# The second mixer of a two-layer trunk: gate products on quarters of the array, ScalarE in the order of issue, and two channel tiles of the output projection tile by tile

## The chip, the cores and the metric

The kernel runs on one core of one Trainium2 chip, in one launch. The metric is the device time in microseconds (us). The kernel before took 1646.99 us (median of three runs, 1646.67 to 1647.06). Its profile comes from one more execution, which took 1642.21 us and whose recorded span is 1640.4 us, with a mean granted TensorE clock of 0.997.

The engines have short names in the profile: PE is TensorE (PEld its weight load), DVE is VectorE, ACT is ScalarE, POOL is GpSimd, and SP is SyncE, which here only issues DMAs.

## The reference

The model has two layers on 256 context tokens and 256 latent tokens with 1024 channels. A layer is a half-step SwiGLU feed-forward block, a mixer, and a second feed-forward block, each between two norms. The change concerns the mixer of the second layer, which gives out latent tokens only. Of its heads it needs three groups, cut here to their core:

```python
# recurrent heads: 512 channels; r, i, a, bx for two directions d, then a linear scan each way
r  = sigmoid(einsum('blhi,hij->blhj', xh, w_r[d]) + b_r[d])     # heads of 64 channels: 64 x 64 blocks
i  = sigmoid(einsum('blhi,hij->blhj', xh, w_i[d]) + b_i[d])
log_a = -8.0 * r * softplus(-lam[d]);  a = exp(log_a)
bx = sqrt(-expm1(2.0 * log_a)) * (i * xf)
h[t] = a[t] * h[t-1] + bx[t]            # context first, then latent; d == 1 runs backward
o_lru = gelu(lru_gate) * (h_forward + h_backward)
# short convolution: 256 channels                # chunk mixing: 256 channels, chunks of 128 tokens
o_sc = sc_bg * conv3(sc_cg * sc_x)
o_cm = gelu(cm_u) * (einsum('hpq,bnqhd->bnphd', ws, gelu(cm_v)) + bs)
out  = concatenate([o_lru, o_sc, o_cm]) @ w_mix_out
```

## The kernel before, in words

Channels lie on the 128 partitions and tokens along the free axis, so 1024 channels are eight channel tiles. A product of the input projection is taken as three: each fp32 weight tile and each activation tile is split into a rounded part `hi` (a cast on ScalarE, line 173) and a rest `lo` (a subtraction on VectorE, line 174), and hi·hi, hi·lo and lo·hi are added. The 2304 projected columns come as 16 units of 128 columns and, for the value half of the chunk mixing, two units that hold half of the contraction each for 256 columns. A unit of 128 is loaded by one DMA, cast by two instructions, subtracted by two, and then takes 24 TensorE instructions.

The middle of the second mixer is a list of parts in ORDER[1], each a letter and a number. `mixer` calls them in that order:

- `c`, `x`, `b`: the three products of a short convolution half, with its work on VectorE (lines 759 to 787).
- `C`: the four-tap convolution of a recurrent channel tile over all 512 tokens (lines 701 and 703).
- `G`: the gates of that tile. Its weights `wbd` are block-diagonal 128 x 128 fp32 matrices of two 64-channel heads; four products of 512 columns each (two directions, r and i), a sigmoid each on ScalarE (lines 719 and 723), and a multiplication on VectorE (724).
- `D`: the decay, exp and tanh on ScalarE (730, 731) and three VectorE instructions per direction (732, 734, 735).
- `S`: root (ScalarE, 741), root times input (742), scans (744, 747, 748), sum and gate (750, 751) on VectorE. The result is one of the inputs `oh[0]` to `oh[3]` of the output projection.
- `v`, `u`, `m`: the chunk mixing. `v` is the value product with two gelus (798), `u` a unit with a gelu (805), `m` a product with `wcm`, an addition and a multiplication on VectorE (816, 818). Its results are `oh[6]` and `oh[7]`; those of the short convolution are `oh[4]` and `oh[5]`.
- `w` loads the output weights of one of eight output tiles; `p` issues the four products of one output tile with `oh[4]` to `oh[7]`.

Behind the list come the products of LATE[0] with that channel tile for all eight output tiles (`out_part`). Then, output tile by output tile, follow the products of LATE[1] and, for each tile, three ScalarE passes over its result (899 to 901), a VectorE product `c` (903), sums, and products with `ones` into `st`, from which the norm is made. After these comes the next feed-forward block.

Two things set the order of the instructions on an engine. For the engines in MANUAL (before: TensorE alone) the instructions stand in the order in which the code issues them. For the other engines a scheduler picks the order when the program is built, and it is then fixed: each engine works through its own list, and an instruction at the head that waits holds all behind it. Each ScalarE function that is in another table than the one loaded costs an ACT_TABLE_LOAD: sigmoid, exp with tanh, gelu and root each bring one when they follow another.

Weights are loaded by SP; `raw` tiles have four buffers (NRAW), split tiles six (NSPL).

Of the kernel before, what the change touches and what calls it, by code (L numbers as in the profile page):

```python
# [34 lines left out]
PARK = {2: 2, 3: 3, 6: 0, 7: 1}  # L35
NTMP = 3
NSQ = 3
JACC = 'gvg'
FIRST = 2

# [3 lines left out]

OUT_AT = ((0, 0), (0, 1), (1, 0), (1, 1), (2, 0), (3, 0), (4, 0), (5, 0))

LATE = ((0,), (1, 2, 3))
MANUAL = {mybir.EngineType.PE}

ORDER = ("c1 C0 g3 G0 C1 C2 C3 D0 c0 x1 G1 G3 D3 x0 S0 D1 v0 S3 G2 b0 g2 D2 u0 m0 S1 b1 u1 m1 S2",  # L50
         "c0 x0 C1 C0 C3 C2 g3 g2 G1 G0 D1 D0 c1 b0 u0 v0 S1 w0 G3 u1 x1 b1 m1 w1 S0 m0 G2 w2 p1 w3 w4 w5 p2 p5 w6 D2 S2 w7 p0 "
         "D3 S3 p7 p4 p3 p6")

TAIL = 4

# [26 lines left out]
def backbone(ctx: ExitStack, tc: tile.TileContext, xT, vecs, crow, w_mod, w_in, w_out, w_mi, w_mo, w_lru, w_cm, b_cm, lam, w_last, out):  # L82
    nc = tc.nc
# [12 lines left out]
    def nm(s):  # L96
        cnt[0] += 1
        return f"{s}_{cnt[0]}"
# [4 lines left out]
    def pbank():  # L103
        return ps.tile([P, 512], F32, tag="mm", name=nm("mm"))
# [525 lines left out]
    def mixer(l, segs, nxt, plan, skew_out, order_of, next_unit=None):  # L630
# [77 lines left out]

        def lru_conv(c):
            xcs[c] = conv(c)  # L710

        def lru_gates(c):
            wbd = tp.tile([P, 4, P], F32, tag="wbd", name=nm("wbd"))
            nc.sync.dma_start(wbd, w_lru[l, c])
            for c, d, b in heads[2 * c:2 * c + 2]:
                pr = pbank()
                pe.matmul(pr, lhsT=wbd[:, 2 * d, :], rhs=xcs[c], start=True, stop=True)
                r = rs[c, d] = tt_()
                sc.activation(r, pr, AF.Sigmoid, bias=V("b_r", b))
                pi = pbank()  # L720
                pe.matmul(pi, lhsT=wbd[:, 2 * d + 1, :], rhs=xcs[c], start=True, stop=True)
                i = ix[c, d] = tt_()
                sc.activation(i, pi, AF.Sigmoid, bias=V("b_i", b))
                ve.tensor_tensor(i, i, xcs[c], op=OP.mult)

        def lru_decay(c):
            for c, d, b in heads[2 * c:2 * c + 2]:
# [7 lines left out]
                ve.tensor_scalar(e, e, -1.0, 1.0, op0=OP.mult, op1=OP.add)  # L735
                es[c, d] = e

        def lru_scan(c):
            for c, d, _ in heads[2 * c:2 * c + 2]:
                e, h, b = es[c, d], rs[c, d], ix[c, d]  # L740
                sc.activation(h, h, AF.Sqrt, scale=-1.0)
                ve.tensor_tensor(b, b, h, op=OP.mult)
                if d == 0:
                    ve.tensor_tensor_scan(h, e, b, 0.0, op0=OP.mult, op1=OP.add)
                else:
                    r1, r2 = slice(SEQ - 1, None, -1), slice(T - 1, SEQ - 1, -1)
                    ve.tensor_tensor_scan(h[:, r1], e[:, r1], b[:, r1], 0.0, op0=OP.mult, op1=OP.add)
                    ve.tensor_tensor_scan(h[:, r2], e[:, r2], b[:, r2], h[:, 0:1], op0=OP.mult, op1=OP.add)
            h = rs[c, 1]
            ve.tensor_tensor(h[:, a0:b0], h[:, a0:b0], rs[c, 0][:, a0:b0], op=OP.add)  # L750
            ve.tensor_tensor(h[:, a0:b0], h[:, a0:b0], gates[c][:, a0:b0], op=OP.mult)
            put(c, h)

        sc_o, sc_p = {}, {}

# [86 lines left out]
        def out_part(k):  # L842
            for m in range(KT):
                out_mm(m, (k,))

        parts = dict(w=out_load, p=lambda m: out_mm(m, (4, 5, 6, 7)), g=gate, c=short_c, x=short_x, b=short_b, v=lambda _: chunk_v(), u=chunk_u, m=chunk_mix,
                     C=lru_conv, G=lru_gates, D=lru_decay, S=lru_scan)
        def issue():
            for part in order_of.split():
                parts[part[0]](int(part[1]))  # L850

        if len(segs) == 2:
            with tc.manual_schedule(engines=MANUAL):
                issue()
            norms = Norms(segs, None, l, 1, nxt)
            order = [4, 5, 6, 7, 0, 1, 2, 3]
            y = norms.y = [tt_() for _ in range(KT)]

            def load(m):
# [11 lines left out]
        need(l, 8)  # L871
        need(nxt[0], 3 * nxt[1])
        need(nxt[0], 3 * nxt[1] + 1)
        with tc.manual_schedule(engines=MANUAL):
# [376 lines left out]
```

## Time and profile before

| | |
|---|---|
| median of three runs | 1646.99 us |
| the profiled execution | 1642.21 us, its span 1640.4 us |
| PE busy | 1612.5 us, 98% of the span |
| DVE, ACT, POOL busy | 1164.3, 736.7, 120.3 us |
| the chain that ended last | PE 89%, DVE 6%, ACT 3% of the span |
| HBM traffic | 247.39 MB read, 151 GB/s over the span |

The stretch that the change touches is the second mixer's middle, about 1350 to 1447 us of the span. In these 97 us PE was busy for 92.57, ACT for 80.60 and DVE for 78.28 us, POOL for 6.43.

How to read it: a row of the timeline gives the start in us, the duration in us, engine, line, operation, out<-in by the program's names with buffer numbers left out, shapes, and xN where N instructions of one kind stand in a row and are shown as one; the duration is then that of all N. What stands in brackets is the idle time before and what ended it. On PE an fp32 product of weight and data shows as two instructions. Consecutive instructions of an engine overlap a little, so what one adds to a row of work is the distance between starts.

### The profile page before, as it was taken

What the parts mean: (1) busy time and instruction counts of PE and PEld (TensorE: products, weight loads), DVE (VectorE), ACT (ScalarE), POOL (GpSimd) and SP (SyncE); (2) the same over time, 40 slices, a digit from 0 to 9 for tenths busy, and PEclk for the clock granted to TensorE, in tenths of its full rate; (3) what the DMA queues carried; (4) which work ended last, traced back from release to release, by engine and by line L of the source; (5) the groups of instructions that cost most, each with busy time, mean ns of one, the idle gap of its engine ahead of it and who ended that gap; (6) DMA issues with size and microseconds to landing.
All of it is one profiled execution on the core that took longest, in us unless ns stands there. A gap on an engine that the chain in (4) does not pass through costs nothing.

```text
span 1640.4 us, 23432 instructions
## 1 busy us (share of the span) xinstructions
PE 1612.5 (98%) x8846; PEld 1371.6 (84%) x8846; DVE 1164.3 (71%) x2183; ACT 736.7 (45%) x1378; POOL 120.3 (7%) x166
## 2 busy tenths in 40 slices
PE   6999999999999999999999999999999999999998
PEld 3788888889977998888888998888888998789997
DVE  4899898548788787867763887767432788785554
ACT  5523322244697662332233462332232479864543
POOL 0000000005000500000000410000000410100000
PEclk9999999999999999999999999999999999999999
DMA  9577677431323225655552215655422316155552
GB/s 370 189 218 261 205 229 223 144 121 44 103 72 120 77 97 187 221 162 174 179 164 80 100 61 194 222 166 167 141 90 90 103 54 210 47 167 194 180 191 78
DMA packets 73906, 249.97 MB, mean 152 GB/s; under 512 B 8384, under 2 KB 10048, under 8 KB 73792
## 3 DMA queue, kind: packets, MB, share of 16 engines
q1 hardware_dynamic: 73216, 247.94, 45.9%
q8 instruction: 69, 1.13, 0.3%
q10 hardware_dynamic: 576, 0.52, 0.1%
q14 instruction: 45, 0.37, 0.1%
HBM read 247.39 MB, written 1.05 MB: 151 GB/s over the span
## 4 chain that ended last, share of the span: by engine, by line
PE 89%; DVE 6%; ACT 3%; DMA 1%; issue 1%; POOL 0%; SPq 0%; POOLq 0%; DVEq 0%; ACTq 0%
PE mm L113 87%; PE st L113 1%; DVE x L271 1%; DVE sq L394 1%; DVE t L703 0%; PE mod L113 0%; DVE z L270 0%; DVE tmp L262 0%; DMA x<-in_xT 0%; ACT hi L173 0%; DVE t L397 0%; POOL rs L241 0%; DVE t L332 0%; DMA raw<-in_w_mi 0%; ACT t L730 0%
## 5 line engine op out<-in xcount | busy, mean ns | idle before, releaser
L173 ACT CAST hi<-raw 128x512 fp32r<-128x512 f32 (+1 forms) x596 | 343.6, 610 | 672.7 <-PE mm L113 475.8
L113 PE MATMUL mm<-hh,hi 128*128 128x512 f32 (+1 forms) x1840 | 625.6, 348 | 0.5 <-ACT hh L1095 0.2
L113 PE MATMUL mm<-hl,hi 128*128 128x512 f32 (+1 forms) x1840 | 622.5, 346 | 1.8 <-DVE hl L256 1.0
L174 DVE TENSOR_TENSOR lo<-raw,hi 128x512 fp32r<-128x512 f32 (+1 forms) x596 | 387.5, 680 | 157.3 <-ACT hi L173 154.5
L113 PE MATMUL mm<-hh,lo 128*128 128x512 f32 (+1 forms) x1840 | 466.6, 346 | 0.0
L113 PEld LDWEIGHTS mm<-hh,hi 128*128 128x128 f32 x1840 | 345.5, 188 | 52.1 <-ACT hh L1095 2.8
L113 PEld LDWEIGHTS mm<-hl,hi 128*128 128x128 f32 x1840 | 345.9, 188 | 51.2 <-DVE hl L1101 1.6
L113 PEld LDWEIGHTS mm<-hh,lo 128*128 128x128 f32 x1840 | 325.1, 188 | 47.2
L196 DVE SCALAR_TENSOR_TENSOR junk<-raw,cb 128x1024 bf16<-128x1024 f32 x256 | 312.9, 1222 | 70.8 <-DMA raw<-in_w_mod 67.1
L113 PE MATMUL mm<-t,hi 128*128 128x512 f32 (+1 forms) x1056 | 240.6, 367 | 0.0
L113 PEld LDWEIGHTS mm<-t,hi 128*128 128x128 f32 x1056 | 182.8, 188 | 35.7 <-issue 0.2
L397 POOL TENSOR_TENSOR t<-t,sq 128x256 f32<-128x256 f32 x112 | 94.2, 856 | 712.2 <-ACT sq L391 702.3
L113 PE MATMUL mm<-t,lo 128*128 128x512 f32 (+1 forms) x528 | 131.5, 367 | 0.0
L113 PEld LDWEIGHTS mm<-t,lo 128*128 128x128 f32 x528 | 92.6, 188 | 17.7
L480 DVE TENSOR_TENSOR sg<-sg,mm 128x512 f32<-128x512 f32 (+1 forms) x72 | 45.9, 640 | 78.3 <-PE mm L113 78.3
L113 PE MATMUL mm<-t,hh 128*128 128x256 f32 x512 | 71.2, 281 | 0.0
L113 PEld LDWEIGHTS mm<-t,hh 128*128 128x128 f32 x512 | 65.7, 188 | 0.5
L173 ACT CAST t<-sg 128x512 fp32r<-128x512 f32 (+1 forms) x94 | 50.6, 541 | 32.0 <-DVE sg L480 29.0
L332 DVE TENSOR_TENSOR t<-t,mm 128x256 f32<-128x256 f32 (+1 forms) x66 | 35.4, 536 | 29.3 <-PE mm L113 29.1
L174 DVE TENSOR_TENSOR t<-sg,t 128x512 fp32r<-128x512 f32 (+1 forms) x94 | 55.3, 589 | 0.9 <-ACT t L173 0.9
L113 PE MATMUL mm<-hi,t 128*128 128x512 f32 x176 | 55.1, 394 | 0.0
L263 ACT ACTIVATE hh<-tmp,modv 128x256 fp32r<-128x256 f32 x72 | 42.4, 596 | 22.1 <-DVE tmp L262 21.9
(179 smaller groups left out, 1212.4 us busy)
## 6 DMA issues: line engine op xcount, KB each, us to landing
raw<-in_w_in SPq DMA_DIRECT2D x176, 512.0 KB, 3.6
raw<-in_w_mod SPq DMA_DIRECT2D x128, 512.0 KB, 4.3
raw<-in_w_out SPq DMA_DIRECT2D x48, 512.0 KB, 3.3
raw<-in_w_mi SPq DMA_DIRECT2D x36, 512.0 KB, 4.1
raw<-in_w_last SPq DMA_DIRECT2D x22, 512.0 KB, 3.3
raw<-in_w_out SPq DMA_DIRECT2D x24, 384.0 KB, 3.7
t<-in_w_mod SPq DMA_DIRECT2D x32, 256.0 KB, 5.8
raw<-in_w_mo SPq DMA_DIRECT2D x8, 512.0 KB, 3.7
```

The lines of the kernel that those rows point to most:

```text
L113: te.matmul(dst, lhsT=lhsT, rhs=rhs, start=start, stop=stop)
L173: sc.copy(hi, src)
L174: ve.tensor_tensor(lo, src, hi.bitcast(F32), op=OP.subtract)
L196: ve.scalar_tensor_tensor(junk, raw.rearrange("p k c -> p (k c)"), 1.0, cb[:, s], op0=OP.mult, op1=OP.mult, accum_out=modv[l][:, v, m, s:s ...
L263: sc.activation(hh[:, m, a:b], tmp, AF.Identity, scale=A, bias=B)
L271: ve.scalar_tensor_tensor(x[:, m, a:b], z, mcol(l, 3 * i + 2, m, s), x[:, m, a:b], op0=OP.mult, op1=OP.add)
L332: ve.tensor_tensor(y[m][:, a:b], y[m][:, a:b], p[:, :b - a], op=OP.add)
L394: ve.scalar_tensor_tensor(q[2], y, G, x[:, m, a:b], op0=OP.mult, op1=OP.mult)
L397: (gp if JACC[c] == "g" else ve).tensor_tensor(acc[c], acc[c], q[c], op=OP.add)
L480: ve.tensor_tensor(sg[:, :b - a], sg[:, :b - a], pu[:, :b - a], op=OP.mult)
```

## The change

Three edits, all for the second layer's mixer; the first layer's instructions keep their order on each engine.

1. Gates on quarters. Instead of a block-diagonal 128 x 128 matrix, `gate_products` keeps only the 64 x 64 blocks and issues two products of 64 rows by 64 columns where there was one. Rows of the array are given by g (0 for r, 1 for i), columns by the head h. For two of the four quarters the head's 64 channels lie on the other half of the partitions, so `lru_swap` makes a copy of the channel tile with its halves exchanged, by two DMAs from GpSimd per channel tile. The weights come in by four DMAs per channel tile, where there was one.
2. ScalarE in the order of issue. IN_ORDER adds ScalarE to TensorE for the second layer; VectorE stays with the scheduler. The roots become a part of their own, `R`, and the hand-over to the output projection another, `H`. ORDER[1] is written anew, so that gates, decays, roots and scans of two channel tiles come together; `l4` fills the queue of units to four.
3. LATE: the products with channel tiles 1 and 0 come ahead for all output tiles, those with 3 and 2 tile by tile (before: 0 ahead, and 1, 2, 3 tile by tile).

```diff
-LATE = ((0,), (1, 2, 3))
+LATE = ((1, 0), (3, 2))
 MANUAL = {mybir.EngineType.PE}
+IN_ORDER = {mybir.EngineType.PE, mybir.EngineType.Activation}
...
-         "c0 x0 C1 C0 C3 C2 g3 g2 G1 G0 D1 D0 c1 b0 u0 v0 S1 w0 G3 u1 x1 b1 m1 w1 S0 m0 G2 w2 p1 w3 w4 w5 p2 p5 w6 D2 S2 w7 p0 "
-         "D3 S3 p7 p4 p3 p6")
+         "c0 x0 C1 C0 C3 C2 g3 g2 G1 G0 c1 l4 D1 D0 b0 R1 R0 S1 S0 H1 H0 u0 u1 v0 G3 G2 D3 D2 w0 x1 b1 R3 R2 S3 S2 H3 H2 "
+         "m1 w1 m0 w2 p1 w3 w4 w5 p2 p5 w6 w7 p0 p7 p4 p3 p6")
...
         def lru_conv(c):
             xcs[c] = conv(c)
+            if l in QUARTERS:
+                lru_swap(c)
...
+        def lru_swap(c):
+            t = turned_xc[c] = tp.tile([P, T], F32, tag="swap", name=nm("swap"), bufs=2)
+            for a, b in ((0, P // 2), (P // 2, 0)):
+                gp.dma_start(t[a:a + P // 2], xcs[c][b:b + P // 2])
...
+            if l in QUARTERS:
+                wbd = tp.tile([P, 2, 2, P // 2], F32, tag="wbd", name=nm("wbd"))
+                for g in range(2):
+                    for h in range(2):
+                        a = 64 * h
+                        src = w_lru[l, c].rearrange("p (d g) o -> p d g o", g=2)
+                        nc.sync.dma_start(wbd[64 * g:64 * g + 64, :, h], src[a:a + 64, :, g, a:a + 64])
+            else:
+                wbd = tp.tile([P, 4, P], F32, tag="swap", name=nm("wbd"))
...
+                    for h in range(2):
+                        src = (xcs if g == h else turned_xc)[c]
+                        rows, cols = slice(64 * g, 64 * g + 64), slice(64 * h, 64 * h + 64)
+                        pe.matmul(p[cols], lhsT=wbd[rows, d, h], rhs=src[rows], start=True, stop=True)
...
+        def lru_root(c):
+            for d in range(2):
+                sc.activation(rs[c, d], rs[c, d], AF.Sqrt, scale=-1.0)
+
         def lru_scan(c):
-            for c, d, _ in heads[2 * c:2 * c + 2]:
+            for d in range(2):
                 e, h, b = es[c, d], rs[c, d], ix[c, d]
-                sc.activation(h, h, AF.Sqrt, scale=-1.0)
...
-            put(c, h)
+
+        def lru_put(c):
+            put(c, rs[c, 1])
...
-        with tc.manual_schedule(engines=MANUAL):
+        with tc.manual_schedule(engines=IN_ORDER if l in QUARTERS else MANUAL):
             issue()
             for k in LATE[0]:
                 out_part(k)
-        with tc.manual_schedule(engines=MANUAL2):
+        with tc.manual_schedule(engines=MANUAL2 | IN_ORDER if l in QUARTERS else MANUAL2):
```

In the order rows below, line numbers of the changed kernel are some 3 higher at its top and 36 to 42 higher in the mixer (741 becomes 777, 744 becomes 784, 747 and 748 become 787 and 788, 750 and 751 become 790 and 791, 816 and 818 become 858 and 860, 174 becomes 177); numbers behind a name tell tiles of one name apart.

First place: VectorE from the end of the scans of channel tile 0 on, in the kernel before. `t_12484` and `t_12503` are the two chunk mixes, `oh[7]` and `oh[6]`; 742 is root times input, 783 belongs to a short convolution.

```order
L742 TENSOR_TENSOR t_12149<-t_12149,t_12145 128x512
L783 TENSOR_TENSOR t_12218<-t_12218,mm_12453 128x256
L816 TENSOR_TENSOR t_12484<-mm_12479,bcm 128x256
L744 SCALAR_TENSOR_TENSOR t_12145<-t_12173,t_12149 128x512
L818 TENSOR_TENSOR t_12484<-t_12484,t_12422 128x256
L742 TENSOR_TENSOR t_12158<-t_12158,t_12154 128x512
L816 TENSOR_TENSOR t_12503<-mm_12498,bcm 128x256
L747 SCALAR_TENSOR_TENSOR t_12154<-t_12179,t_12158 128x256
L818 TENSOR_TENSOR t_12503<-t_12503,t_12287 128x256
L748 SCALAR_TENSOR_TENSOR t_12154<-t_12179,t_12154,t_12158 128x256
L750 TENSOR_TENSOR t_12154<-t_12154,t_12145 128x256
```

The same place in the changed kernel, which is the end of the scans of channel tiles 3 and 2. Its chunk mixes are `t_12595` (`oh[7]`) and `t_12605` (`oh[6]`).

```order
L790 TENSOR_TENSOR t_12459<-t_12459,t_12448 128x256
L782 TENSOR_TENSOR t_12488<-t_12488,t_12486 128x512
L791 TENSOR_TENSOR t_12459<-t_12459,t_12096 128x256
L787 SCALAR_TENSOR_TENSOR t_12486<-t_12509,t_12488 128x256
L858 TENSOR_TENSOR t_12595<-mm_12590,bcm 128x256
L788 SCALAR_TENSOR_TENSOR t_12486<-t_12509,t_12486,t_12488 128x256
L860 TENSOR_TENSOR t_12595<-t_12595,t_12366 128x256
L790 TENSOR_TENSOR t_12486<-t_12486,t_12475 128x256
L858 TENSOR_TENSOR t_12605<-mm_12600,bcm 128x256
L791 TENSOR_TENSOR t_12486<-t_12486,t_12131 128x256
L860 TENSOR_TENSOR t_12605<-t_12605,t_12331 128x256
```

Before, the chunk mixes stood between the scans of channel tile 0, ahead of all work of the decays of tiles 2 and 3; now they stand between the last scans of all, and the second one's multiplication is the last row of them.

Second place: VectorE around the rests of the second unit of `v`, in the kernel before. They are the rows of `lo_12257`; the first unit's are those of `lo_12223`, and line 732 begins the first decay.

```order
L174 TENSOR_TENSOR lo_12223<-raw_12220,hi_12222 128x512
L724 TENSOR_TENSOR t_12149<-t_12149,t_12036 128x512
L174 TENSOR_TENSOR lo_12223<-raw_12220,hi_12222 128x512
L174 TENSOR_TENSOR lo_12257<-raw_12254,hi_12256 128x512
L724 TENSOR_TENSOR t_12158<-t_12158,t_12036 128x512
L174 TENSOR_TENSOR lo_12257<-raw_12254,hi_12256 128x512
L174 TENSOR_TENSOR lo_12292<-raw_12289,hi_12291 128x512
L732 SCALAR_TENSOR_TENSOR t_12161<-t_12161,t_12125 128x512
```

In the changed kernel they are the rows of `lo_12336`.

```order
L787 SCALAR_TENSOR_TENSOR t_12155<-t_12244,t_12157 128x256
L784 SCALAR_TENSOR_TENSOR t_12171<-t_12250,t_12173 128x512
L788 SCALAR_TENSOR_TENSOR t_12155<-t_12244,t_12155,t_12157 128x256
L782 TENSOR_TENSOR t_12184<-t_12184,t_12182 128x512
L790 TENSOR_TENSOR t_12155<-t_12155,t_12144 128x256
L787 SCALAR_TENSOR_TENSOR t_12182<-t_12256,t_12184 128x256
L791 TENSOR_TENSOR t_12155<-t_12155,t_11837 128x256
L788 SCALAR_TENSOR_TENSOR t_12182<-t_12256,t_12182,t_12184 128x256
L177 TENSOR_TENSOR lo_12336<-raw_12333,hi_12335 128x512
L790 TENSOR_TENSOR t_12182<-t_12182,t_12171 128x256
L177 TENSOR_TENSOR lo_12336<-raw_12333,hi_12335 128x512
```

They stood ahead of the first decay, and now stand behind it and behind all scans of channel tiles 1 and 0 but the last two short instructions.

Third place: ScalarE from the first gelus of the chunk mixing on, in the kernel before.

```order
L805 ACT_TABLE_LOAD
L805 ACTIVATE t_12287<-mm_12262 128x256
L741 ACT_TABLE_LOAD
L741 ACTIVATE t_12125<-t_12125 128x512
L798 ACT_TABLE_LOAD
L798 ACTIVATE t_12330<-mm_12305 128x256
L741 ACT_TABLE_LOAD
L741 ACTIVATE t_12134<-t_12134 128x512
L798 ACT_TABLE_LOAD
L798 ACTIVATE t_12330<-mm_12332 128x256
L719 ACT_TABLE_LOAD
```

ScalarE in the changed kernel, from the roots of channel tiles 1 and 0 to the gelus of `v` (line 840) and the next sigmoid table; `hi_12335` is the second unit of `v`.

```order
L777 ACTIVATE t_12155<-t_12155 128x512
L777 ACTIVATE t_12171<-t_12171 128x512
L777 ACTIVATE t_12182<-t_12182 128x512
L847 ACT_TABLE_LOAD
L847 ACTIVATE t_12331<-mm_12306 128x256
L176 CAST hi_12335<-raw_12333 128x512 x2
L847 ACTIVATE t_12366<-mm_12341 128x256
L176 CAST hi_12370<-raw_12368 128x512 x2
L176 CAST hi_12378<-raw_12376 128x512 x2
L840 ACTIVATE t_12409<-mm_12384 128x256
L840 ACTIVATE t_12409<-mm_12411 128x256
L758 ACT_TABLE_LOAD
```

Gelus and roots alternated, each with its table; now the four roots stand together, then the gelu of `u` and the casts of three units, then the other gelus. The cast of the second unit of `v` has moved behind the roots. From the first sigmoid table to the last root there were 15 table loads and are now seven.

## Rows read from the trace of the kernel before

**Rows 1.** The page: the chain that ended last, by engine.
```profile
PE 89%; DVE 6%; ACT 3%; DMA 1%; issue 1%; POOL 0%; SPq 0%; POOLq 0%; DVEq 0%; ACTq 0%
```

**Rows 2.** Timeline of PE, second mixer: start, us, operation; brackets: idle before.
```profile
1362.54 7.03 PE L113 MATMUL mm<-t,wbd 128*128 128x512 f32 x16
...
1375.08 0.28 PE L113 MATMUL mm<-hh,hi 128*128 128x256 f32 x1
...
1377.92 0.28 PE L113 MATMUL mm<-hi,hh 128*128 128x256 f32 x1
...
1396.06 1.09 PE L113 MATMUL mm<-wcm,t 128*64 128x128 f32 x16
...
1401.88 17.53 PE L113 MATMUL mm<-t,wo 128*128 128x256 f32 x80 [0.23 <-DVE t L818]
1420.17 3.26 PE L113 MATMUL mm<-t,wo 128*128 128x256 f32 x14 [0.76 <-DVE t L751]
```

**Rows 3.** Timeline of ACT, second mixer.
```profile
1363.14 1.28 ACT L719 ACT_TABLE_LOAD   x1
...
1365.02 0.68 ACT L723 ACTIVATE t<-mm,vec 128x512 f32<-128x512 f32 x1
...
1370.92 0.68 ACT L723 ACTIVATE t<-mm,vec 128x512 f32<-128x512 f32 x1
...
1372.91 1.34 ACT L730 ACTIVATE t<-t,s 128x512 f32<-128x512 f32 x2
...
1377.84 0.35 ACT L759 COPY t<-mm 128x256 f32<-128x256 f32 x1
1378.09 1.66 ACT L173 CAST hi<-raw 128x512 fp32r<-128x512 f32 x3
...
1408.54 1.15 ACT L741 ACTIVATE t<-t 128x512 f32<-128x512 f32 x2
...
1411.74 1.28 ACT L741 ACT_TABLE_LOAD   x1
...
1422.18 0.38 ACT L899 ACTIVATE t<-mm 128x256 f32<-128x256 f32 x1 [0.16 <-PE mm L113]
```

**Rows 4.** Timeline of DVE, second mixer: decays and scans.
```profile
1374.90 1.31 DVE L732 SCALAR_TENSOR_TENSOR t<-t,t 128x512 f32<-128x512 f32 x2 [1.37 <-ACT t L731]
...
1381.08 0.41 DVE L783 TENSOR_TENSOR t<-t,mm 128x256 f32<-128x256 f32 x1
...
1397.17 0.69 DVE L742 TENSOR_TENSOR t<-t,t 128x512 f32<-128x512 f32 x1 [0.95 <-ACT t L741]
...
1398.44 1.22 DVE L744 TENSOR_TENSOR_SCAN t<-t,t 128x512 f32<-128x512 f32 x1
...
1400.83 0.68 DVE L747 TENSOR_TENSOR_SCAN t<-t,t 128x256 f32<-128x256 f32 x1
...
1401.74 0.75 DVE L748 TENSOR_TENSOR_SCAN t<-t,t,t 128x256 f32<-128x256 f32 x1
1402.52 0.42 DVE L750 TENSOR_TENSOR t<-t,t 128x256 f32<-128x256 f32 x1
...
1403.32 1.28 DVE L724 TENSOR_TENSOR t<-t,t 128x512 f32<-128x512 f32 x2
...
1419.61 0.42 DVE L751 TENSOR_TENSOR t<-t,t 128x256 f32<-128x256 f32 x1
```

**Rows 5.** Windows around the mixer's end: busy time by engine, PEclk, DMA share, GB/s.
```profile
1436.00:1437.00 1.00, 0.25 (x3) 0.25 (x3) 0.79 (x2) 0.18 (x1) 0.00 (x0) 1.00 0.55 94
1437.00:1438.00 1.00, 1.00 (x9) 1.00 (x8) 0.90 (x2) 0.00 (x0) 0.00 (x0) 0.70 0.92 344
1438.00:1444.00 6.00, 5.75 (x27) 5.33 (x26) 3.82 (x15) 1.99 (x4) 2.29 (x2) 0.50 0.45 153
```

**Rows 6.** Timeline of PE near the start, a product of 32 stationary columns.
```profile
34.54 1.93 PE L113 MATMUL mod<-t,cs 128*32 128x512 f32 x16
```

**Rows 7.** DMA issues, 1320 to 1400 us: KB each, median us to landing.
```profile
wbd<-in_w_lru SPq DMA_DIRECT2D x2, 256.0 KB, 3.9
```

More of the change, by code (lines that the diff above doesn't have):

```diff
@@ L37 @@
 NSQ = 3
+QUARTERS = (1,)
 JACC = 'gvg'
@@ L45 @@
 OUT_AT = ((0, 0), (0, 1), (1, 0), (1, 1), (2, 0), (3, 0), (4, 0), (5, 0))
-LATE = ((0,), (1, 2, 3))
+LATE = ((1, 0), (3, 2))
 MANUAL = {mybir.EngineType.PE}
-ORDER = ("c1 C0 g3 G0 C1 C2 C3 D0 c0 x1 G1 G3 D3 x0 S0 D1 v0 S3 G2 b0 g2 D2 u0 m0 S1 b1 u1 m1 S2",
-         "c0 x0 C1 C0 C3 C2 g3 g2 G1 G0 D1 D0 c1 b0 u0 v0 S1 w0 G3 u1 x1 b1 m1 w1 S0 m0 G2 w2 p1 w3 w4 w5 p2 p5 w6 D2 S2 w7 p0 "
-         "D3 S3 p7 p4 p3 p6")
+IN_ORDER = {mybir.EngineType.PE, mybir.EngineType.Activation}
+ORDER = ("c1 C0 g3 G0 C1 C2 C3 D0 c0 x1 G1 G3 D3 x0 R0 S0 H0 D1 v0 R3 S3 H3 G2 b0 g2 D2 u0 m0 R1 S1 H1 b1 u1 m1 R2 S2 H2",
+         "c0 x0 C1 C0 C3 C2 g3 g2 G1 G0 c1 l4 D1 D0 b0 R1 R0 S1 S0 H1 H0 u0 u1 v0 G3 G2 D3 D2 w0 x1 b1 R3 R2 S3 S2 H3 H2 "
+         "m1 w1 m0 w2 p1 w3 w4 w5 p2 p5 w6 w7 p0 p7 p4 p3 p6")
 TAIL = 4
@@ L710, in lru_conv, with gate_products, products @@
             xcs[c] = conv(c)
+            if l in QUARTERS:
+                lru_swap(c)
+        turned_xc = {}
+        def lru_swap(c):
+            t = turned_xc[c] = tp.tile([P, T], F32, tag="swap", name=nm("swap"), bufs=2)
+            for a, b in ((0, P // 2), (P // 2, 0)):
+                gp.dma_start(t[a:a + P // 2], xcs[c][b:b + P // 2])
+        def gate_products(c):
+            if l in QUARTERS:
[7 more added lines that the diff above has]
+                wbd = tp.tile([P, 4, P], F32, tag="swap", name=nm("wbd"))
+                nc.sync.dma_start(wbd, w_lru[l, c])
+            def products(d):
+                ps2 = pbank(), pbank()
+                for g, p in enumerate(ps2):
+                    if l not in QUARTERS:
+                        pe.matmul(p, lhsT=wbd[:, 2 * d + g, :], rhs=xcs[c], start=True, stop=True)
+                        continue
+                    for h in range(2):
+                        src = (xcs if g == h else turned_xc)[c]
+                        rows, cols = slice(64 * g, 64 * g + 64), slice(64 * h, 64 * h + 64)
+                        pe.matmul(p[cols], lhsT=wbd[rows, d, h], rhs=src[rows], start=True, stop=True)
+                return ps2
+            return products
         def lru_gates(c):
-            wbd = tp.tile([P, 4, P], F32, tag="wbd", name=nm("wbd"))
-            nc.sync.dma_start(wbd, w_lru[l, c])
+            products = gate_products(c)
             for c, d, b in heads[2 * c:2 * c + 2]:
-                pr = pbank()
-                pe.matmul(pr, lhsT=wbd[:, 2 * d, :], rhs=xcs[c], start=True, stop=True)
+                pr, pi = products(d)
                 r = rs[c, d] = tt_()
                 sc.activation(r, pr, AF.Sigmoid, bias=V("b_r", b))
-                pi = pbank()
-                pe.matmul(pi, lhsT=wbd[:, 2 * d + 1, :], rhs=xcs[c], start=True, stop=True)
                 i = ix[c, d] = tt_()
@@ L846, in mixer @@
         parts = dict(w=out_load, p=lambda m: out_mm(m, (4, 5, 6, 7)), g=gate, c=short_c, x=short_x, b=short_b, v=lambda _: chunk_v(), u=chunk_u, m=chunk_mix,
-                     C=lru_conv, G=lru_gates, D=lru_decay, S=lru_scan)
+                     C=lru_conv, G=lru_gates, D=lru_decay, R=lru_root, S=lru_scan, H=lru_put, l=fill)
         def issue():
@@ L873, in mixer @@
         need(nxt[0], 3 * nxt[1] + 1)
-        with tc.manual_schedule(engines=MANUAL):
+        with tc.manual_schedule(engines=IN_ORDER if l in QUARTERS else MANUAL):
             issue()
```

## The prediction, made before the changed kernel ran

> **What bounds the kernel now.** I read the chain of waits first, for the engine that carries the end, then the timelines of PE, ACT and DVE over the second mixer, and last the windows at its end for the clock. The chain lies on PE for 89% of the span [rows 1]: time is lost where PE stands still or runs slower, and gained where it has less to do. In the second mixer PE hardly stands still: the last bracket before the output products is 0.23 us, behind a chunk mix (line 818), and the next 0.76 us, behind the last gate multiplication of a scan (line 751) [rows 2]. The reader should see why: while ACT and DVE work on the second pair of channel tiles, until 1420.0 [rows 4], PE has 80 instructions of output products to do, 17.53 us of them [rows 2]. That cover is what the change touches. ACT is busy at the same time, and 15 table loads of 1.28 us lie between its first sigmoid and its last root, the first at 1363.14 and the last at 1411.74 [rows 3].
>
> **What the change does, part by part.** I follow the changed order through the stretch with durations of the trace, from 1363.14, where the first sigmoid table is loaded, since all ahead of it is the same work in the same order.
>
> *First pair of gates.* Before, 16 instructions took 7.03 us [rows 2], 0.44 each, and the last sigmoid stood at 1370.92 [rows 3]. Now there are 64 (32 quarter products) of as many columns. The trace has no product of 64 rows. It has products on part of the columns: 16 instructions with 32 stationary columns and 512 moving ones took 1.93 us [rows 6], where one after another 16 x 0.44 = 7.0 would be due, so nearly four ran at once; 16 with 64 stationary columns and 128 moving ones took 1.09 us [rows 2], against 16 x 0.11 = 1.8 by the same price. So parts of the array work beside each other; whether parts of its rows do is open. Bounds for two channel tiles: 64 x 0.44 / 4 = 7.0 / 2 = 3.5 us if four go at once, 7.0 if two do, 14.1 if none. I take 3.5, since the rows of products on part of the columns are the nearest. The sigmoids then bound it: table until 1364.4, eight at 0.6 from start to start (the second starts at 1365.02 [rows 3]), end at 1369.2.
>
> The Trainium skill, TensorEngine Tiling (Array Packing), Key Properties, says that tiles of the array work independently of each other but that a change of tiling mode drains the engine. Rows 6 agree on the first for columns, and by it the gates take 3.5 us, as taken; by the second rule the sum would have some drains more, at the entry and the end of each group of gates, for which no row gives a price.
>
> The exchanged copies come over GpSimd's queue, of which the trace has no row. The nearest is the gate weights' 256 KB in 3.9 us [rows 7]; a copy has as much in two DMAs, is issued behind its convolution and has until the gates' turn. I take nothing, bounds 0 to +4. The split weight loads, some now ahead of other weights on SP's queue, I put at 0, bounds -1 to +1: a DMA of 256 KB in 3.9 us goes for four of 64 KB.
>
> *First decays and roots.* Behind the sigmoids stand six casts and a copy on ACT: 6 x 0.56 + 0.25 = 3.6 [rows 3], end 1372.8, about 1373 with a wait for weights. Table 1.28, eight exp and tanh at (1377.84 - 1372.91) / 8 = 0.62, or 5.0 [rows 3]: 1379.3. Table, four roots at 0.58: 1382.9. That is earlier than before, when the roots alternated with gelus. Then table, a gelu and two casts, 1.28 + 0.4 + 1.1: the second unit of `v` is cast at 1385.7.
>
> *The first loss.* Its rest on DVE stands behind the scans. Twelve decay instructions take 1381.08 - 1374.90 = 6.2 us [rows 4]; they begin with the first tanh, at about 1376, and end at 1382.2. From there to the first `lo` of that unit there are four multiplications (line 742's kind), two long and four half scans, and two short instructions. From start to start these cost 0.61, 1.14, 0.60, 0.75 and 0.4 [rows 4], so 2.4 + 2.3 + 1.2 + 1.5 + 0.8 = 8.2: the first half at 1390.4, the second, behind one short instruction, done at 1392. PE reaches that unit in its value product with nothing else to issue, so it stands still from about 1381 to 1391 but for its first products. A unit's 24 products take 2.84 us (1375.08 to 1377.92, [rows 2]); two of them, with the first units' part already done, end at 1396.1.
>
> *Second pair.* Behind the gelu of `v` ACT's list has the sigmoids of G3 and G2, and since ACT now keeps the order of issue, none can go ahead: gelu 1396.5, table and eight sigmoids at 0.6 until 1402.6, table and eight exp and tanh until 1408.9, table and four roots until 1412.5. DVE has its twelve decay instructions from 1405.1 on and three of the short convolution: 6.2 + 1.1, so the first root's multiplication is at 1412.4.
>
> *The second loss.* Both chunk mixes stand behind or between these last scans in DVE's list. The stretch from there to the last chunk multiplication: before, the scans of one channel tile, both chunk mixes and a short instruction took 1403.32 - 1397.17 = 6.15 us [rows 4]; less 0.35 for the short one and plus 4.3 for a second channel tile (2 x 0.61 + 1.14 + 0.60 + 0.68 + 0.7), 10.1: DVE is done at 1422.5. PE's third output product needs `oh[6]`, that is, just that last row. So of the 48 products that were to lie beside the scans (`p` for eight tiles, then channel tiles 1 and 0) 46 start at 1422.5. An instruction is 17.53 / 80 = 0.22 us [rows 2], a product two: 46 x 0.43 = 19.7, until 1442.2. Four more products, two for each of the first two output tiles, 1.7, and the first pass over an output tile comes at 1444.0. Before it came at 1422.18 [rows 3]: +21.8.
>
> That is how the sum stands to the diff: eight table loads fewer save 8 x 1.28 = 10.2 us of ACT, but DVE's last scan ends later than before (1422 against 1420.0) and the cover of 17.5 us is now behind it, not beside it.
>
> *Output tile by tile.* Two products each in place of three: 8 x 0.43 = 3.4 less on PE. ACT's three passes bound this phase as well, so I take -1, bounds 0 and -3.4.
>
> *Clock.* In the window from 1436 to 1437 PE was busy for 0.25 of 1 us; the granted clock then fell to 0.70 and for six us to 0.50, the lower of its two levels, 1.2 GHz [rows 5], although PE was busy again. That cost 0.3 + 3.0 = 3.3 us. The change makes two such gaps, ten and fifteen us long (1381 to 1391, 1407 to 1422), each followed by products that carry the end: twice 3.3 is 6.6. I take 5, bounds 0 and 6.6.
>
> The Trainium skill, TensorE: Matmul & The Clock Gate, section HAM oscillation, says the same of kernels that wait between bursts of products: each burst begins cold. Rows 5 show one such case. The rule speaks against this change: by it both bursts pay in full and the sum has 6.6 here.
>
> Sum: 21.8 - 1 + 5 = +25.8. On the profiled execution: 1642.2 + 25.8 = 1668.0. The median of the runs shown is 1646.99, 4.8 above it, so 1672.8; I say 1673.
>
> **Rivals.**
> 1. *Quarters two at a time.* Each pair of gate groups takes 7.0 us, and the last sigmoid stands where it did: 1371.6 in place of 1369.2, twice, about +5: 1677. For it: two quarters of one product share a row group of the array, the other two the other, and the trace has concurrency only among columns. Against: nothing but the rows 6, which are of another kind.
> 2. *Quarters one after another.* Then 14.1 us per pair, of which the sigmoids hide 4.8; each pair ends some 8 later, +16: 1688 to 1690. Rows 2 and 6 speak against it.
> 3. *Faster.* The chunk mixes reach PE before the scans end, because the work of `m1` and `m0` on DVE comes early enough not to hold `p` back. Then PE takes channel tiles 1 and 0 too under the last scans, and behind them it has two products for each output tile left where it had three: 8 x 0.43 = 3.4, and ACT's chain with fewer tables would end the scans some 3 to 4 earlier: about -7, 1640. It decides if the second chunk mix is done before about 1400. Against it: DVE's list is fixed, and its last row of the scans is the second chunk mix.
> 4. *No change.* Gains and losses cancel within 0.2% (3.3 us, about what the measurement can tell): it would need the first loss without the second, or a much shorter one.
>
> **How the numbers follow.** The forecast, with quarters four at a time, has 0.62; rival 1 0.20, rival 2 0.08, rival 3 0.04, rival 4 0.02; the rest, 0.04, are mixtures that are slower too. The forecast's own bounds are 21.8 - 3.4 + 0 = +18.4 (1665) and 21.8 + 6.6 = +28.4, with the copies' 4 some +32 (1679). Rival 1 with its clock's bound ends at 1681, and five us more for waits that I have not seen gives 1686; below, five us for a shorter second loss give 1660. Faster by over 0.2% has 0.04, within 0.2% 0.02, slower 0.94.
>
> **What would show it.** In the changed kernel's trace: a PE gap before the value product's second unit that ends with a DVE `lo`; a second gap of ten us or more before the third output product, ended by DVE's chunk multiplication; 92 output instructions in a row behind it; a granted clock near 0.50 behind each gap; gate groups of 3.5 us. The forecast is wrong if output products lie beside the last scans, or if the sigmoids of the second pair start well before 1396.

## The result: 1.4 to 1.7% slower, by two places in the lists of ScalarE and VectorE

The changed kernel took 1670.95 us (median of four runs, 1668.71 to 1671.14), the kernel before 1646.83 in the same comparison: a ratio of 1.0143, 95% interval 1.0126 to 1.0161, or 24.1 us more where 26 were forecast. On a second chip the ratio was 1.0167 (1.0151 to 1.0182). The execution with the profile took 1668.71 us, 26.5 more than that of before.

Here is the middle of the second mixer in the changed kernel, first ScalarE's timeline. It answers [rows 3].

```profile
1361.76 1.28 ACT L758 ACT_TABLE_LOAD   x1
...
1367.06 0.73 ACT L760 ACTIVATE t<-mm,vec 128x512 f32<-128x512 f32 x1
...
1378.33 1.28 ACT L777 ACT_TABLE_LOAD   x1
...
1381.83 1.28 ACT L847 ACT_TABLE_LOAD   x1
...
1383.41 1.13 ACT L176 CAST hi<-raw 128x512 fp32r<-128x512 f32 x2
...
1396.47 0.38 ACT L840 ACTIVATE t<-mm 128x256 f32<-128x256 f32 x1 [3.26 <-PE mm L116]
...
1409.83 1.28 ACT L777 ACT_TABLE_LOAD   x1
1411.12 2.19 ACT L777 ACTIVATE t<-t 128x512 f32<-128x512 f32 x4
1447.62 0.38 ACT L941 ACTIVATE t<-mm 128x256 f32<-128x256 f32 x1 [34.31 <-PE mm L116]
...
1467.87 0.60 ACT L266 ACTIVATE hh<-tmp,modv 128x256 fp32r<-128x256 f32 x1 [3.31 <-DVE tmp L265]
```

The first sigmoid table is loaded at 1361.76 (1363.14 before), the first pass over an output tile starts at 1447.62, 85.86 us later, where it was 59.04. From the table on, the whole way is 26.8 us longer. ScalarE itself is done with its last root at 1413.3 and then waits 34 us. The last row is the beginning of the next feed-forward block, its first `hh` (the rounded part of its activation tile), which in the kernel before is this row:

```profile
1443.63 0.60 ACT L263 ACTIVATE hh<-tmp,modv 128x256 fp32r<-128x256 f32 x1 [2.12 <-DVE tmp L262]
```

TensorE's timeline, to be held against [rows 2]; a 64 x 64 product shows as 64*64.

```profile
1361.25 0.64 PE L116 MATMUL mm<-t,wbd 64*64 64x512 f32 x1
1361.26 0.64 PE L116 MATMUL mm<-swap,wbd 64*64 64x512 f32 x1
...
1365.62 0.38 PE L116 MATMUL mm<-hh,hi 128*128 128x256 f32 x1
...
1384.07 0.58 PE L116 MATMUL mm<-hi,hh 128*128 128x256 f32 x1 [5.89 <-ACT hi L176]
1389.13 0.58 PE L116 MATMUL mm<-lo,hh 128*128 128x256 f32 x1 [4.48 <-DVE lo L177]
...
1396.37 0.64 PE L116 MATMUL mm<-t,wbd 64*64 64x512 f32 x1
1396.37 0.65 PE L116 MATMUL mm<-swap,wbd 64*64 64x512 f32 x2
1396.38 1.05 PE L116 MATMUL mm<-t,wbd 64*64 64x512 f32 x2
...
1400.49 0.39 PE L116 MATMUL mm<-hh,hi 128*128 128x256 f32 x1
```

From the first gate product to the next other product it is 4.4 us for the first pair of channel tiles and 4.1 for the second.

The same engine from the chunk mixing's products on:

```profile
1407.39 0.70 PE L116 MATMUL mm<-t,wo 128*128 128x256 f32 x2
1413.15 1.22 PE L116 MATMUL mm<-t,wo 128*128 128x256 f32 x2 [5.07 <-DVE t L825]
1422.91 25.54 PE L116 MATMUL mm<-t,wo 128*128 128x256 f32 x104 [8.54 <-DVE t L860]
```

The two waits ahead of the value product, 5.89 us for a cast and 4.48 us for its rest, are the first loss; 5.07 and 8.54 us ahead of the output products are the second. Behind the last one stand 104 output instructions in a row; 92 of them are the 46 products that were to lie beside the scans. The cast is ScalarE's, behind the roots in its list. The other three waits end with rows of VectorE: the rest of `v`'s second unit (line 177), a product of the short convolution (825) and the second chunk mix (860). Its timeline shows the first and the last of these:

```profile
1380.29 0.69 DVE L782 TENSOR_TENSOR t<-t,t 128x512 f32<-128x512 f32 x1
...
1388.41 0.67 DVE L177 TENSOR_TENSOR lo<-raw,hi 128x512 fp32r<-128x512 f32 x1
...
1389.33 0.68 DVE L177 TENSOR_TENSOR lo<-raw,hi 128x512 fp32r<-128x512 f32 x1
...
1420.15 0.40 DVE L858 TENSOR_TENSOR t<-mm,bcm 128x256 f32<-128x256 f32 x1
...
1421.12 0.40 DVE L860 TENSOR_TENSOR t<-t,t 128x256 f32<-128x256 f32 x1
...
1421.78 0.41 DVE L858 TENSOR_TENSOR t<-mm,bcm 128x256 f32<-128x256 f32 x1
...
1422.44 0.41 DVE L860 TENSOR_TENSOR t<-t,t 128x256 f32<-128x256 f32 x1
```

VectorE multiplied the first root at 1380.29, came to the unit's rest at 1388.41, and to the last chunk multiplication, the last row of its list there, at 1422.44.

The granted clock in windows of the changed kernel (busy time of PE, PEclk, DMA share, GB/s), against [rows 5]:

```profile
1381.00:1384.00 3.00, 0.00 (x0) 0.50 0.00 0
1391.00:1394.00 3.00, 3.00 (x16) 0.50 0.84 231
1416.00:1420.00 4.00, 0.00 (x0) 0.50 0.00 0
1423.00:1425.00 2.00, 2.00 (x5) 0.50 0.00 0
1429.00:1432.00 3.00, 3.00 (x16) 1.00 0.00 0
1464.00:1468.00 4.00, 2.54 (x12) 0.50 0.38 112
1468.00:1474.00 6.00, 4.97 (x22) 0.50 0.15 61
1476.00:1480.00 4.00, 4.00 (x34) 0.94 0.02 4
```

It fell to 0.50 in each gap and stayed there for the first us of the products behind it: from 1389 to 1394 and from 1423 to 1428. The third fall is the one that [rows 5] show at the mixer's end. There it was over when the next block began; here it lasts until 1476, eight us into that block, which began at 1467.87 (1443.63 before). From that point to the end of the span it is 199.0 us, before 196.8.

### The profile page after: what moved, and what is told of

Same layout as the page of the kernel before. It is cut to its first block, busy times and chain, and to the rows that moved or that the text cites. A ratio compares the mean times of both kernels' runs of the same rounds, so it can differ in the third digit from the quotient of the medians.

```text
span 1666.9 us, 23526 instructions
## 1 busy us (share of the span) xinstructions
PE 1616.5 (97%) x8878; PEld 1375.4 (83%) x8878; DVE 1163.0 (70%) x2183; ACT 726.3 (44%) x1370; POOL 124.4 (7%) x174
## 4 chain that ended last, share of the span: by engine, by line
PE 90%; DVE 6%; ACT 2%; issue 1%; DMA 1%; POOL 0%; SPq 0%; POOLq 0%; DVEq 0%; ACTq 0%
PE mm L116 88%; PE st L116 1%; DVE x L274 1%; DVE sq L397 1%; DVE t L706 0%; DVE z L273 0%; PE mod L116 0%; DVE tmp L265 0%; DVE t L400 0%; DMA x<-in_xT 0%; DVE t L771 0%; DVE t L782 0%; DVE t L769 0%; DVE t L784 0%; DMA raw<-in_w_mi 0%
## 5 line engine op out<-in xcount | busy, mean ns | idle before, releaser
L116 PEld LDWEIGHTS mm<-t,lo 128*128 128x128 f32 x528 | 92.5, 188 | 17.7
```

The costliest lines, as they stand in the source:

```text
L116: te.matmul(dst, lhsT=lhsT, rhs=rhs, start=start, stop=stop)
```

## The experiments

Ratios are to the kernel before on the same chip, with 95% intervals. For the middle of the mixer I give two distances from each profile, which leave out what happens before and behind: from the first sigmoid table to the first pass over an output tile, and to the next block's first `hh`. They are 59.0 and 80.5 us before, 85.9 and 106.1 in the changed kernel. The changed kernel itself did not run beside the first eight experiments. Its own ratios, from two other comparisons, are 1.0143 and 1.0167, so a difference of under 4 us between one of these experiments and the changed kernel is not shown by time.

**Chunk mixes ahead of the last scans.**

```diff
-b1 R3 R2 S3 S2 H3 H2 m1 w1 m0 w2
+b1 R3 R2 m1 m0 S3 S2 H3 H2 w1 w2
```

> One edit to the changed kernel: in ORDER[1] the chunk mixes m1 m0 are issued ahead of the scans S3 S2, so that VectorE's list has them behind the decays and ahead of the last scans; TensorE's and ScalarE's lists stay as they are. Theory (the second loss is the place of the chunk mixes in VectorE's list): VectorE is through with the decays at about 1412.7 in the changed kernel's trace, two additions and two multiplications take 1.4 us, so the 46 output products start at about 1414.5 in place of 1422.9, and the gap before them shrinks from 8.5 us to about 1: 8 us less, some 1663. Rival (the loss lies in ScalarE's order or the clock, and the mixes only show it): the products start earlier but the first pass over an output tile stays within 2 us of 1447.6, and the time stays at 1669 to 1671.

Ratio 1.0121 (1.0103 to 1.0139). TensorE's timeline at the output products:

```profile
1416.40 26.04 PE L116 MATMUL mm<-t,wo 128*128 128x256 f32 x106 [5.07 <-DVE t L825]
```

Windows of that kernel from there on (busy time of PE, PEclk, DMA share, GB/s):

```profile
1420.00:1425.00 5.00, 5.00 (x20) 0.82 0.00 0
1425.00:1440.00 15.00, 15.00 (x71) 1.00 0.00 0
1440.00:1445.00 5.00, 4.05 (x21) 1.00 0.00 0
1445.00:1450.00 5.00, 5.00 (x18) 0.57 0.35 110
1450.00:1455.00 5.00, 5.00 (x18) 0.50 0.00 0
1455.00:1460.00 5.00, 5.00 (x24) 0.50 0.32 105
1460.00:1465.00 5.00, 4.99 (x23) 0.50 0.31 105
```

The gap of 8.5 us is gone, and the first pass comes after 76.8 us, 9.1 earlier. By this the theory holds. To the next block it is 102.8 us, only 3.3 less: from 1445 on the granted clock was 0.50 until about 1473, through all output tiles, although PE was busy for nearly all of the last four windows. So 5.8 us of the gain were given back in this profile, by the clock and not by a wait. The other three executions took 1661.24 to 1665.46 us, the profiled one 1667.13. By time the kernel is 20 us slower than the kernel before, where the changed kernel is 24 to 27: of the 8 us expected, 4 to 7.

**The second unit of `v` cast ahead of the decays.** `l5` fills the queue of units to five.

```diff
-G1 G0 c1 l4 D1 D0
+G1 G0 c1 l5 D1 D0
```

> One edit to the changed kernel: l5 for l4 in ORDER[1], so that the second unit of v is loaded and cast ahead of the first decays. Theory (the first loss is the place of that unit behind roots and scans): TensorE takes the value product without the gaps of 5.9 and 4.5 us, two units of 2.84 us end near 1387 to 1389 in place of 1396, and the second pair of gates and all behind it come some 7 us earlier, of which a cast more ahead of the decays takes 1 back: 6 to 8 us less, 1663 to 1665. The second gap, before the third output product, stays as long as it is. Rival (the second pair is bound by ScalarE's own work, so that the unit's place hides behind it): under 2 us.

Ratio 1.0108 (1.0093 to 1.0123); distances 77.2 and 98.6 us, so 8.7 and 7.5 less. The waits ahead of the value product are gone; two shorter ones, 2.14 and 1.27 us for gelus, now stand ahead of the second gates. The wait for the chunk mix, which was expected to stay as long, grew to 13.46 us, since TensorE came to it earlier:

```profile
1416.06 24.27 PE L116 MATMUL mm<-t,wo 128*128 128x256 f32 x104 [13.46 <-DVE t L860]
```

**Both.** The two edits above together.

> Both edits to the changed kernel, chunk mixes ahead of the last scans and the second unit of v cast ahead of the decays. Theory: two losses in a row on one chain, so they add: 14 to 16 us less than the changed kernel, 1655 to 1657, still slower than the kernel before by some 8 to 10, because the decays of the second pair still stand ahead of the mixes and TensorE has nothing to do then. Rival (one loss hides the other): no better than the better of the two single edits by more than 2 us.

Ratio 1.0087 (1.0071 to 1.0102); 72.3 and 92.5 us, 13.6 less each; by time it is 9 to 13 less, where 14 to 16 were expected. The two losses add, but not in full (8.7 and 9.1 make 17.8): a wait for the second chunk mix is left, which now stands behind the decays.

```profile
1409.89 25.53 PE L116 MATMUL mm<-t,wo 128*128 128x256 f32 x104 [5.63 <-DVE t L860]
```

What is left to the kernel before, 13.2 us, shows for the most part in the same profile: waits of 2.58 and 1.27 us for gelus, the 5.63 us, and 25.53 us for 104 instructions that take 22.7 where the clock doesn't fall (TensorE kept busy, below). Between 1390 and 1400 the granted clock was 0.57 as well; what that cost was not measured.

**The quarters alone.** The changed kernel with LATE, ORDER[1] (the new letters R and H beside S) and ScalarE's scheduling as before.

```diff
-LATE = ((1, 0), (3, 2))
+LATE = ((0,), (1, 2, 3))
...
-IN_ORDER = {mybir.EngineType.PE, mybir.EngineType.Activation}
+IN_ORDER = {mybir.EngineType.PE}
...
+"c0 x0 C1 C0 C3 C2 g3 g2 G1 G0 D1 D0 c1 b0 u0 v0 R1 S1 H1 w0 G3 u1 x1 b1 m1 w1 R0 S0 H0 m0 G2 ...
```

> The quarters alone: the changed kernel with LATE, ScalarE's scheduling and the order of the parts as in the kernel before (the roots issued just ahead of their scans). Theory: the quarters took 4.4 and 4.1 us for two channel tiles where the full array took 7.0 to 7.3, with no wait for the swapped copies, so they save TensorE some 5.5 us in all; the scans' end is set by ScalarE and VectorE and moves less, so 0 to 4 us less than the kernel before, 1643 to 1647, with the 80 output instructions again beside the scans. Rival (the quarters or their swaps are what costs the time): slower than the kernel before by 2 us or more.

Ratio 0.9988 (0.9977 to 0.9999), so a gain at the edge of the interval. It was run again with more executions:

> The kernel with the quarters alone once more, beside the reordered one on the same chip. Theory: 1 to 3 us less than the kernel before, as in the first comparison (0.9988). Rival (that comparison was within the scatter): the interval takes in 1.

Ratio 1.0000 (0.9989 to 1.0011): the rival holds, there is no gain that can be measured. TensorE's timeline of this second run says where the time of the gates went:

```profile
1384.59 0.38 PE L115 MATMUL mm<-hh,hi 128*128 128x256 f32 x1 [2.08 <-ACT t L839]
...
1392.47 0.39 PE L115 MATMUL mm<-hh,hi 128*128 128x256 f32 x1 [0.41 <-ACT hi L175]
```

At the output products of the same kernel:

```profile
1401.31 17.53 PE L115 MATMUL mm<-t,wo 128*128 128x256 f32 x80 [1.49 <-DVE t L859]
1419.48 3.26 PE L115 MATMUL mm<-t,wo 128*128 128x256 f32 x14 [0.64 <-DVE t L790]
```

TensorE now waits 2.08 us for a gelu of `v`, 0.41 for a cast and 1.49 for a chunk mix, together 4.0 us, where before there were two of 0.23. From the first gate product to the third output product TensorE was busy for 35.30 us in place of 38.89 and idle for 4.0 in place of 0.45, and both stretches are 39.3 us long. The granted clock in it was 0.96 (before 1.00), so the rest of the 5.5 us may lie there. The wait for the last scan ends 56.9 us behind the first table, as before (57.0). ScalarE's 15 table loads and VectorE's scans set that end, and the quarters don't touch them.

**TensorE kept busy in the second gap.**

```diff
-m1 w1 m0 w2 p1
+m1 w1 m0 w2 z0 p1
...
+        def busy(_):
+            p = pbank()
+            for _ in range(16):
+                te.matmul(p, lhsT=ident, rhs=x[:, 0, :], start=True, stop=True)
...
```

> The changed kernel with 16 more fp32 products of 512 columns on TensorE, issued behind the chunk mixing's products and ahead of the first output products; their result is read by nothing. At 0.85 us each they fill 1407.4 to 1421, inside the wait that ended at 1422.9, and wait for nothing. Theory (the clock is a loss of its own beside the wait): the granted clock does not fall in that stretch, the 104 output instructions take 22.2 us (104 x 0.2135) in place of 25.5, and the time is 3 to 5 us less than the changed kernel's, 1666 to 1668. Rival (the clock falls for other reasons, or the products get in the way): the granted clock is 0.50 there as before, no gain, or some us slower.

The timeline of TensorE:

```profile
1410.89 14.00 PE L891 MATMUL mm<-x,ident 128*128 128x512 f32 x32
...
1426.43 22.71 PE L116 MATMUL mm<-t,wo 128*128 128x256 f32 x104 [0.67 <-DVE t L860]
```

The granted clock did not fall there, and the 104 instructions took 22.71 us in place of 25.54. From the table to the first pass it is 83.8 us, 2.0 less, to the next block 105.2, 0.9 less. The ratio, 1.0163 (1.0133 to 1.0194), lies between the two of the changed kernel: by time, the gain of 3 to 5 us is not shown. By the 104 instructions the clock's part behind that gap is 2.8 us where 3.3 were expected, and the rest of the loss there is the wait itself.

**ScalarE left to the scheduler.**

```diff
-IN_ORDER = {mybir.EngineType.PE, mybir.EngineType.Activation}
+IN_ORDER = {mybir.EngineType.PE}
```

> The changed kernel with ScalarE left to the scheduler in the second mixer too (IN_ORDER holds TensorE alone); quarters, order of the parts and LATE stay. In its lists the rests of the second unit of v stand ahead of the first decays on VectorE, and the chunk mixes stand behind the last scan. Theory (two losses on one chain, the first from ScalarE's order): the first goes, the second stays: TensorE's value product ends some 7 us earlier, the gap before the output products stays or grows, in all 6 to 9 us less than the changed kernel, 1661 to 1664. Rival (the order of issue on ScalarE is the whole loss): back to 1650 or below.

Ratio 1.0111 (1.0084 to 1.0138); distances 76.2 and 97.0 us, 9.6 and 9.2 less. The first loss is gone as with the cast ahead of the decays. The second stands without ScalarE's order of issue too, so that order is not its cause:

```profile
1404.81 1.22 PE L116 MATMUL mm<-t,wo 128*128 128x256 f32 x2 [5.91 <-DVE t L825]
1414.10 25.55 PE L116 MATMUL mm<-t,wo 128*128 128x256 f32 x104 [8.06 <-DVE t L860]
```

**Full-width gates in the changed order.** `gate_products` takes the full-array branch in both layers, and the copies are left out.

```diff
         def lru_conv(c):
             xcs[c] = conv(c)
-            if l in QUARTERS:
-                lru_swap(c)
...
-            if l in QUARTERS:
+            if l in ():
                 wbd = tp.tile([P, 2, 2, P // 2], F32, tag="wbd", name=nm("wbd"))
...
-                    if l not in QUARTERS:
+                    if True:
```

> The changed kernel with the gates of the second mixer as products of the full array again (one weight DMA per channel tile, no swapped copies); order of the parts, ScalarE's order and LATE stay as changed. Theory (quarters save time on the chain): each pair of gate groups takes 7.0 us again in place of 4.4 and 4.1, the sigmoids wait for it, the last of each pair comes 2 to 2.5 us later: 3 to 5 us slower than the changed kernel, 1673 to 1676. Rival (quarters, swaps or their DMAs cost): faster than the changed kernel by 2 us or more.

Ratio 1.0188 (1.0162 to 1.0215); 89.2 and 109.6 us, 3.4 and 3.5 more. Each pair of gates took 7.03 us again:

```profile
1368.27 7.03 PE L116 MATMUL mm<-t,wbd 128*128 128x512 f32 x16
```

The last sigmoid of each pair comes 1.1 us later behind its table than in the changed kernel, where 2 to 2.5 were expected, and the copy behind the first pair (line 799) waits 1.12 us for TensorE. Where the gates stand on the chain, then, the quarters are worth 3.4 us by this profile; by time, 1.0188 against 1.0143 and 1.0167, 3 to 7 us.

**LATE alone, in the kernel before.**

```diff
-LATE = ((0,), (1, 2, 3))
+LATE = ((1, 0), (3, 2))
```

> The kernel before with one line changed, LATE = ((1, 0), (3, 2)). Theory: the eight products with channel tile 1 move ahead of the tile by tile phase, 8 x 0.43 = 3.4 us; before, TensorE waited only 0.76 us there for the last scan, so that phase begins up to 2.7 us later, and it is shortened by some 1 us only, since ScalarE's three passes bind it too: 0 to 2.5 us slower than the kernel before. Rival (LATE alone is a gain): 2 us or more faster.

Ratio 1.0024 (1.0012 to 1.0036), or 4 us; expected was at most 2.5. The first pass comes 1.9 us later (61.0 us) and the next block 0.8 (81.3), as the theory has it; the rest I have only from the granted clock, which over this kernel's executions was 0.990 to 0.996 and over those of before 0.992 to 0.997. Why it falls more often here is open, and what LATE does in the changed kernel no run shows by itself.

**The list in another order.**

```diff
-LATE = ((1, 0), (3, 2))
+LATE = ((0,), (1, 2, 3))
-"c0 x0 C1 C0 C3 C2 g3 g2 G1 G0 c1 l4 D1 D0 b0 R1 R0 S1 S0 H1 H0 u0 u1 v0 G3 G2 D3 D2 w0 x1 b1 R3 R2 S3 S2 H3 H2 "
-"m1 w1 m0 w2 p1 ...
+"c0 x0 C1 C0 C3 C2 g3 g2 G1 G0 c1 l5 D1 D0 b0 l5 u0 v0 u1 x1 R1 R0 m1 m0 S1 S0 H1 H0 b1 G3 G2 D3 D2 w0 R3 R2 S3 S2 H3 H2 "
+"w1 w2 p1 ...
-        with tc.manual_schedule(engines=MANUAL2 | IN_ORDER if l in QUARTERS else MANUAL2):
+        with tc.manual_schedule(engines=MANUAL2):
```

> The changed kernel with another list in ORDER[1], LATE as in the kernel before, and the output tiles under the orders they had before (ScalarE's in order only in the middle): quarters, ScalarE's order of issue and the roots in groups stay. The chunk mixes stand ahead of all scans, u and v ahead of the roots, the short convolution's units are cast ahead of them (l5 twice), the second gates come behind the first scans. Theory (the change lost by where its list put two things, not by the quarters or by ScalarE's order of issue): no wait of TensorE over 3 us between the first gates and the output tiles, the output products beside the last scans, and from the first sigmoid table to the first pass over an output tile 56 to 59 us, against 59.0 before and 85.9 in the changed kernel; 1 to 3 us less than the kernel before. Rival (ScalarE in the order of issue costs by itself, whatever the list): slower than the kernel before by 3 us or more.

Ratio 1.0007 (0.9996 to 1.0018): quarters and ScalarE's order of issue stay, and all 24 to 27 us are back. The distances are 57.7 and 78.5 us, 1.3 and 2.0 less than before; there is one wait of 3.89 us, for the short convolution's product (line 824), a little over the bound expected:

```profile
1403.26 23.02 PE L115 MATMUL mm<-t,wo 128*128 128x256 f32 x98 [3.89 <-DVE t L824]
```

The time doesn't show the 2 us. The granted clock over its twelve executions was 0.991 to 0.997, lower than that of before in many of them; I take that for the reason, but no run separates it. The rival, that ScalarE in the order of issue costs by itself whatever the list, has fallen for the middle of the mixer. But three things differ here from the changed kernel, the list, LATE and the scheduling of the output tiles, and no run parts them; LATE alone cost about 4 us in the kernel before. No kernel here beats the kernel before.

**The changed kernel again.**

> The changed kernel itself beside the others on the same chip: 23 to 26 us slower than the kernel before, ratio 1.014 to 1.016, if the two chips of the earlier runs agree; a ratio under 1.012 would shrink what the single edits gave back.

Ratio 1.0167 (1.0151 to 1.0182), a little above what was expected; distances 86.3 and 106.6 us, within 0.6 of the first profile.

## Why the prediction was right, point by point

The chain was followed from the first sigmoid table, which in this execution came 1.4 us earlier than before; the times below are behind that table, as the prediction has them and as measured.

- *First gates and decays.* Last sigmoid done at +6.1, measured 6.0; exp table at +9.9, measured 9.7; roots done at +19.8, measured 20.1. The quarters took 4.4 us for two channel tiles and 4.1 for the second two, where 3.5 were taken and 7.0 or 14.1 were the rivals' terms. The prediction counted 64 instructions for this; there are 32 (16 quarter products), and its sum comes to 3.5 only because it halves once more than its count gives. What the quarters took beyond 3.5 cost nothing, since the sigmoids of both pairs follow their table without a gap, 0.57 us from start to start. The copies cost nothing either: they landed 2.7 us behind their issue (median of eight, 2.2 to 4.2), the first gate product came without a wait, and one weight load waited 0.3 us for a copy. The split weight loads are of 32 KB, not 64, and landed after 3.7 us.
- *First loss.* The unit's second half done at +28.9, measured 28.3; the last gelu of `v` done at +33.4, measured 35.1. The first half of the rest was done at +27.3 in both; from there on it is 1.7 us more, made up of two things. Of the two units' 48 instructions 39 were still to do, where the sum has all 48, 1.1 us too many at 2.84 / 24 each. And the 39 took 7.24 us (1389.13 to 1396.37) where that price gives 4.6, with the granted clock at 0.50 from 1389 to 1394: 2.7 us for the clock.
- *Second pair and second loss.* Last chunk multiplication done at +59.4, measured 61.1, which carries the 1.7 on. From the first root's multiplication to there it was 9.8 us where 10.1 were worked out.
- *Output products.* From there to the first pass 21.5 us were summed without the clock, and 24.8 measured; 2.8 of the difference is the clock, as the run with TensorE kept busy shows.
- *Sum.* 21.8 and the clock's 5 make 26.8 more at the first pass; 26.8 were measured. The clock took 2.7 and 2.8, so 5.5 where 5 were taken. The 1.1 us of value products counted too many take the other way, and 0.5 us more behind the last chunk multiplication make up the rest, so the exact agreement is luck.
- *Output tiles.* -1 was taken; to the next block it was 21.45 us before and 20.25 now, -1.2. ScalarE in order has a part in it: the broadcast of the second norm waited 1.46 us for POOL, before 0.25, because a `lo` on VectorE waited for a cast behind a copy; with the output tiles' old scheduling the wait was 0.44.
- *What was not in it.* Behind the first `hh` it took 2.3 us more, which I put down to the clock's third fall, since it reached into that block; and the start of the span happened to be 1.4 us shorter; together +0.9, and with them and the output tiles 26.5 in all.
- *Signs.* The gap before the value product's second unit ended with a `lo`, as said, but its larger part, 5.89 us, ended with the cast. The second gap, ten us or more in one, came as two: 5.07 us ended by the short convolution's product, of which the prediction says nothing, and 8.54 ended by the chunk multiplication. The output products did not lie beside the last scans, apart from the two that came first.

The rivals: quarters two or one at a time are refuted by the 4.4 us, and no change by the 24 us. The faster case asked for the second chunk mix before about 1400; it was done at 1422.85. What the Trainium skill's rule on draining between tiling modes (TensorEngine Tiling (Array Packing), Key Properties) costs would lie in the difference between 3.5 and 4.4 us at most; no run shows it by itself. The Trainium skill's rule on the clock (TensorE: Matmul & The Clock Gate, HAM oscillation), that a burst behind a wait begins cold, agrees with the trace: both bursts began at 0.50. The 6.6 that the prediction works out with it compare with 5.5 measured.

## What to carry to other kernels

When the parts of a kernel are put in another order, or one engine is put under the order of issue and another left to a scheduler, read the other's list anew: what it holds last may be what the busiest engine needs first. Work that the busiest engine does beside a chain of other engines costs nothing as long as the chain takes longer; an edit that shortens the chain but lets that work slip behind it pays for the whole of it. Saved time on an engine comes back as a wait where another sets the end, as most of the quarters' 5.5 us did.

## What the runs showed of the hardware

- Quarters of the array work beside each other across its rows too: 32 instructions of 512 columns took 4.4 us for two channel tiles, where 16 of the full array take 7.03. One after another 32 would take 14.1, so a little over three ran at once in the mean, and a quarter takes half of the columns, so across the columns alone no more than two could. In the second pair four start within 0.07 us of 1396.37, two on `t` and two on `swap`.
- The scatter of this kernel's time goes with the granted clock of the execution. Of 23 executions of the kernel before on one chip, eleven at 0.997 took 1642.3 us in the mean, three at 0.994 took 1646.5, and one at 0.992 took 1648.3. Differences of 2 us can't be told from this by few runs, and 0.9988 became 1.0000 when it was run again.
- The granted clock stayed at 0.50 for some 27 us in the first experiment, though TensorE was busy with output tiles for nearly all of them; in the changed kernel the same tiles ran at 1.00 from 1448 to 1460. What decides between the two is open.
- A DMA that copies 128 KB within SBUF, issued by GpSimd, landed after 2.7 us (median of eight) and held GpSimd for about 0.5 us.
